# A gate block moved from beside the state output to the start of the glu stage

## The chip, the cores and the metric

The kernel runs on one core of one Trainium2 chip. The metric is device time in microseconds (us) of one launch. The engines are named as the profile names them: PE (TensorE; PEld are its weight loads), ACT (ScalarE), DVE (VectorE), POOL (GpSimd) and SP (SyncE, which here issues nearly all DMAs, in its own order).

## The reference

One inference step of a two-layer hybrid backbone over 128 context and 1024 latent tokens. Cut to what matters here, a layer does this:

```
h = rmsnorm(x, norm_g) * (1 + scale) + shift
a_in, a_gate, f_in, f_gate, q, k, v, c_gate = split(h @ w_in)
ya, finals = s5_mixer(a_in, ...)              # state-space branch, two directions
za = gelu(ya) @ glu_w
ya = za[..., :512] * sigmoid(za[..., 512:])   # the glu stage
yf = fourier_mix(f_in) @ fnet_w
yc = blocked_attention(q, k, v)
branches = stack([ya * silu(a_gate), yf * silu(f_gate), yc * silu(c_gate)])
g = sigmoid(h @ merge_w + merge_b)            # the gates: 3 x 1024 columns
merged = sum(g * einsum(branches, w_branch))
x + gate * (merged @ w_out)
```

The gates `h @ merge_w` need only `h`, so their blocks can be computed at any point of the layer before the branches are merged.

## The kernel before

Activations are kept transposed: 1152 tokens lie along the free dimension in three chunks of 384 (j = 0, 1, 2), channels on the partitions. A dense product is done in blocks of 128 output columns. Each block is a record in a list (weights, right-hand side, evacuation); `dense(n)` takes the next n blocks. Every product is made of three passes with operands split in a high and a low part (`whi`, `wlo` for weights, `hh`, `hl` for h), so four 128-row slices of a weight are 12 matmuls of 384 columns: a **half-chunk**. A gate block (1024 rows) is 6 half-chunks, two for each token chunk; `dense` yields after each. The weights of half a block are one unit: SP loads it into one of four `wst` tiles, ACT makes `whi`, POOL makes `wlo`, and only then is the `wst` tile free for a later load. The products of a chunk gather in one of two PSUM tiles named `pd`; a third chunk can't start before the evacuation of the first.

`drive` interleaves several such generators by weights, `beside(a, b, n)` runs n steps of b after each step of a. Written out so, the work then goes through a scheduler which fixes one order for each engine; the engines run their orders independently and wait on semaphores.

Two neighbouring stages are touched, once in each layer.

**State output** (pool "o"): `ssm_out_gen` goes through eight groups i. For each it makes coefficients on DVE, POOL and ACT (`ss_CA`, `ss_o`, `ss_CK`), a Toeplitz product on PE (`toeplitz`, 16 small matmuls `pt<-ss_CK,ss_B`), evacuates that (`ss_KV` on ACT and DVE), writes it to DRAM (`tpd`), reads it back in another layout (`ss_TT`) and reorders it on ACT (`ss_TP`). One step later `out_gen` uses `ss_TP` as weights: 12 matmuls (`pa` or `pv` from `ssU,ss_TP` and `ss_Hg,ss_CA`), the gelu on ACT (`ss_Y`), and after every second group the DMAs `ydp` and `ydl` that write y to DRAM. Six blocks of gate 0 (`gate_block(0, b, tha)`, evacuated by ACT into a `jo` tile and stored as `tha`) run between these pieces.

**Glu** (pool "u"): `zload_landed` issues 20 DMAs that read y back into twelve `yl` tiles, lets some half-chunks pass, and then makes the high and low copies (`A<-yl` on ACT and on DVE), four of the twelve after each further half-chunk. Beside it runs one block of gate 1 (stored as `thb`). Then come eight glu blocks (`pd<-A,...`, three half-chunks each, alternately evacuated as `th` by ACT and as `jo<-th,pd` by DVE), driven together with `ada_side_gen`, which loads `aw` (512 KB each, three tiles) and accumulates on DVE (`aacc<-aw`, four operations for each load).

Of the kernel before, what the change touches and what calls it, by code (L numbers as in the profile page):

```python
# [89 lines left out]
QT = 20  # L90


def drive(*gens):
    live = [[0.0, g, float(t)] for g, t in gens]
    while live:
        e = min(live, key=lambda x: x[0])
        try:
            e[0] += (next(e[1]) or 1.0) / e[2]
        except StopIteration:
            live.remove(e)  # L100


class Program:
# [1197 lines left out]
    def zload_landed(self, z_d, zf, tag):  # L1301
        ts = []
        for j in range(3):
            for b in range(4):
                t = self.sb(tag, [128, 384], bufs=12, pool=self.gp)
                self.dma_rows(z_d, b, j, t, False)
                ts.append((j, b, t))
        for _ in range(3):
            yield 1
        for i, (j, b, t) in enumerate(ts):  # L1310
            s = slice(384 * j, 384 * j + 384)
            self.act(zf[:, 0, b, s], t)
            self.tt(zf[:, 1, b, s], t, zf[:, 0, b, s].bitcast(F), OP.subtract)
            if i % 4 == 3:
                yield 1
# [40 lines left out]
    def layer(self, l, cs):  # L1356
# [4 lines left out]
        a_d, y_d = ((dt_(n + "p", (512, SP)), dt_(n + "l", (512, SL))) for n in ("ad", "yd"))  # L1361
# [10 lines left out]
        zt = {}  # L1372
# [127 lines left out]
        run = self.run_all  # L1500
# [3 lines left out]
        with self.spool:  # L1504
            with self.epool:
                if l == 0:
                    with self.pool("gp", l, "s"):
                        drive((self.dense(4), 40), (self.ssm_setup_gen(l), 3))
                else:
                    run(self.dense(4))  # L1510
                if l == 0:
                    for k in range(KD):
                        self.dma(self.xT_d[0][128 * k:128 * k + 128, :], self.xT0[:, k])
                with self.pool("gp", l, "m"):
                    drive((self.dense(4), 47), (self.state_gen(l, a_d), 29))
            with self.pool("qp", l):
                with self.pool("gp", l, "q"):
                    self.qkt = self.qkv_tables(l)
                    def qkv():
                        yield from self.qkv_gen(l, qs_d, k_d, v_d, (0,))  # L1520
                        yield from self.qkv_gen(l, qs_d, k_d, v_d, (1,))
                    q = qkv()
                    self.run_some(q, 8)
                    drive((self.scan_gen(l), 103), (self.dense(12), 140))
                    drive((q, 78), (self.dense(2), 21))
                    self.finals(l)
                with self.pool("gp", l, "o"):
                    drive((self.dense(6), 12*6), (self.ssm_out_gen(l, a_d, y_d), 33), (self.qtail_gen(), QT))
        with self.pool("gp", l, "u"):
            zt["y"] = self.sb("A1", [128, 2, 4, NT], R)  # L1530
            run(self.beside(self.zload_landed(y_d, zt["y"], "yl"), self.dense(1), 1))
            drive((self.dense(8), 47), (self.ada_side_gen(l, self.gp, (4, 5)), 6))
        with self.pool("gp", l, "f"):
            self.fnet_tables()
# [81 lines left out]
    def run(self):  # L1616
        self.open_ssm(0)
        cs = self.cs0 = ExitStack()
        self.np_ = cs.enter_context(self.tc.tile_pool(name="np", bufs=1))
        self.xp = cs.enter_context(self.tc.tile_pool(name="xp", bufs=1))  # L1620
        self.prew = []
        self.setup()
        self.xT0 = xT = self.sb("A1", [128, KD, NT])
        ssq = self.ssq = self.sb("ssqt", [128, 2, 9], pool=self.xp)
        self.rb = {}
        self.xr0 = self.sb("xr0", [128, KD, 384], pool=self.xp)
        ada = self.ada_first_gen(0, self.xp, (2, 0, 3, 1))
        xg = self.xg = self.x_gen(xT, ssq)
        next(ada)
        self.run_some(xg, 6)  # L1630
        self.h_tiles((0,))
        self.rb_first(ssq, 0)
        for k in range(KD):
            self.xr_first(xT, k)
        next(ada)
        next(ada)
        for k in range(4):
            self.h_first(xT, 0, k)
        next(ada)
        next(ada)  # L1640
        for k in range(4, 8):
            self.h_first(xT, 0, k)
        self.run_all(ada)
        for l in range(DEPTH):
            with ExitStack() as cs:
                xT, acc = self.layer(l, cs)
                if l + 1 < DEPTH:
                    self.run_all(self.h_gen(l + 1, xT, acc, (2,)))
                else:
                    self.run_all(self.final_gen(xT, acc, (2,)))  # L1650
# [25 lines left out]
```

## Time and profile before

| | |
|---|---|
| median of 3 runs | 2706.3 us (2704.84 to 2707.11) |
| profiled execution, its own time | 2705.34 us |
| span of that execution in the profile | 2703.5 us |
| PE busy | 2598.1 us, 96% of the span |
| DVE, ACT, POOL busy | 1752.9, 1205.0, 666.8 us |
| state output, layer 0 and layer 1 | about 466 to 574 and 1785 to 1896 us |
| glu stage, layer 0 and layer 1 | about 574 to 640 and 1896 to 1962 us |

Every time inside the kernel is counted from the start of the span. Of the 1.84 us between the profiled execution's own time and its span nothing is seen in the trace. The rows of the trace stand in a section of their own below.

### The profile page before, as it was taken

To read this page: it belongs to the slowest core of one execution; us is meant where nothing else is said; L and a number is where in the kernel's file an instruction comes from. 1 tells how busy PE (TensorE), PEld (TensorE's weight loads), DVE (VectorE), ACT (ScalarE), POOL (GpSimd) and SP (SyncE) were. 2 spreads that over 40 slices of the span, in tenths; PEclk is the share of its full clock that TensorE was granted. 3 is DMA by queue.
4 is the path that set the end of the run, shared out by engine and by line. 5 is a ranking of instruction groups with operands and counts; after the bars stand their busy time and mean duration, and the time that the engine had idled before them with its cause. 6 is when DMAs were issued, how large, how long until landed. Compare 5 with 4: busy or idle time off the path is not lost. (4 is left out here: it accounts for less than half of the span.)

```text
span 2703.5 us, 44530 instructions
## 1 busy us (share of the span) xinstructions
PE 2598.1 (96%) x16093; PEld 2496.0 (92%) x16093; DVE 1752.9 (65%) x3837; ACT 1205.0 (45%) x2762; POOL 666.8 (25%) x526
## 2 busy tenths in 40 slices
PE   7999999999999999999999999989999999999998
PEld 4899999899999899999989999979999998999998
DVE  5759964545478889847463798564654787891443
ACT  4562245742355565423345322565223656543244
POOL 2432122312320120222333322232222202101223
PEclk8999999999999999999999999999999999999999
DMA  7633233565443435535542322345646334442234
GB/s 251 199 102 99 86 112 110 168 191 190 157 131 117 141 120 154 186 94 140 170 131 82 116 86 81 119 139 158 209 143 192 104 116 152 146 123 89 89 119 148
DMA packets 463316, 368.95 MB, mean 136 GB/s; under 512 B 72864, under 2 KB 435960, under 8 KB 462712
## 3 DMA queue, kind: packets, MB, share of 16 engines
q1 hardware_dynamic: 461672, 361.78, 43.8%
q0 software_dynamic: 1424, 4.33, 0.5%
q8 instruction: 127, 2.08, 0.3%
q14 instruction: 93, 0.76, 0.1%
HBM read 245.61 MB, written 120.39 MB: 135 GB/s over the span
## 5 line engine op out<-in xcount | busy, mean ns | idle before, releaser
L169 PE MATMUL pd<-hh,whi 128*128 128x384 f32 x2496 | 855.2, 343 | 9.6 <-ACT jo L143 4.9
L169 PE MATMUL pd<-hh,wlo 128*128 128x384 f32 x2496 | 843.6, 338 | 8.3 <-POOL wlo L146 8.1
L169 PE MATMUL pd<-hl,whi 128*128 128x384 f32 x2496 | 840.4, 337 | 1.0 <-DVE hl L150 1.0
L146 POOL TENSOR_TENSOR wlo<-wst,whi 128x512 fp32r<-128x512 f32 x320 | 445.4, 1394 | 1529.9 <-ACT whi L143 1429.7
L169 PEld LDWEIGHTS pd<-hh,whi 128*128 128x128 f32 x2496 | 470.9, 189 | 16.3 <-ACT jo L143 6.5
L169 PEld LDWEIGHTS pd<-hh,wlo 128*128 128x128 f32 x2496 | 470.7, 189 | 14.9 <-POOL wlo L146 13.8
L169 PEld LDWEIGHTS pd<-hl,whi 128*128 128x128 f32 x2496 | 471.2, 189 | 3.8 <-DVE hl L150 2.6
L169 PE MATMUL pd<-A,whi 128*128 128x384 f32 x1728 | 457.1, 341 | 7.0 <-ACT jo L143 6.1
L143 ACT ACTIVATE whi<-wst 128x512 fp32r<-128x512 f32 x320 | 200.6, 630 | 284.7 <-PE pd L169 185.3
L169 PEld LDWEIGHTS pd<-A,whi 128*128 128x128 f32 x1728 | 310.1, 189 | 9.9 <-ACT jo L143 6.7
L169 PE MATMUL pd<-A,wlo 128*128 128x384 f32 x864 | 293.2, 339 | 0.0
L1118 DVE TENSOR_REDUCE at_mx<-pa 128x1 f32<-128x1152 f32 x128 | 173.3, 1354 | 16.0 <-PE pa L169 15.6
L143 ACT ACTIVATE at_PT<-pt 128x384 fp32r<-128x384 f32 (+1 forms) x260 | 114.9, 490 | 143.2 <-PE pt L174 142.8
L169 PE MATMUL pa<-at_K,at_Q 128*128 128x384 f32 x768 | 167.4, 347 | 8.1 <-ACT at_P L143 5.7
L143 ACT ACTIVATE at_P<-pa,at_mx 128x1152 f32<-128x1152 f32 x128 | 158.1, 1235 | 20.5 <-DVE at_mx L1118 19.3
L169 PEld LDWEIGHTS pd<-A,wlo 128*128 128x128 f32 x864 | 162.9, 189 | 0.1
L169 PEld LDWEIGHTS pa<-at_K,at_Q 128*128 128x128 f32 x768 | 128.2, 188 | 28.8 <-ACT at_P L143 25.1
L169 PE MATMUL pt<-qkW,hh 128*128 128x384 f32 x576 | 149.8, 341 | 0.8 <-DVE qk_xn L146 0.8
L169 PE MATMUL pv<-at_PT,at_V 128*128 128x256 f32 x1152 | 148.7, 283 | 0.0
L169 PEld LDWEIGHTS pv<-at_PT,at_V 128*128 128x128 f32 x1152 | 144.7, 191 | 0.8
L143 ACT ACTIVATE jo<-pd 128x384 f32<-128x384 f32 x120 | 58.0, 485 | 189.8 <-PE pd L169 103.2
L146 DVE TENSOR_TENSOR at_PT<-pt,at_PT 128x384 fp32r<-128x384 f32 (+1 forms) x260 | 133.1, 551 | 9.8 <-ACT at_PT L143 9.1
(297 smaller groups left out, 3713.5 us busy)
## 6 DMA issues: line engine op xcount, KB each, us to landing
aw<-in_ada_w_dram SPq DMA_DIRECT2D x48, 512.0 KB, 4.8
wst<-in_merge_w_dram SPq DMA_DIRECT2D x96, 256.0 KB, 3.0
wst<-in_w_in_dram SPq DMA_DIRECT2D x88, 256.0 KB, 3.0
td<-jo SPq DMA_DIRECT2D x96, 192.0 KB, 1.9
jt<-td SPq DMA_DIRECT2D x96, 192.0 KB, 2.6
wst<-in_w_out_dram SPq DMA_DIRECT2D x64, 256.0 KB, 2.9
sgd<-jo SPq DMA_DIRECT2D x72, 192.0 KB, 1.9
jt<-sgd SPq DMA_DIRECT2D x64, 192.0 KB, 3.0
```

The source lines that it names most:

```text
L143: return self.nc.scalar.activation(out, in_, func, **kw)
L146: return (e or self.nc.vector).tensor_tensor(out=out, in0=a, in1=b, op=op)
L169: return self.nc.tensor.matmul(out, w, x, start=first, stop=last, **kw)
L1118: nc.vector.tensor_reduce(out=mx[:, 0:1], in_=src, axis=AX.XY if m3 else AX.X, op=OP.max, negate=True)
```

## The change

In each layer the state output runs beside five blocks in place of six; its weight in `drive` falls from 72 to 60, so a block is worth the same as before. The sixth block (gate 0, b = 7) is taken by the glu stage, which now has two blocks beside the read-back of y; and the copies of y are written two half-chunks further on.

```
@@ -1305,7 +1305,7 @@
                 t = self.sb(tag, [128, 384], bufs=12, pool=self.gp)
                 self.dma_rows(z_d, b, j, t, False)
                 ts.append((j, b, t))
-        for _ in range(3):
+        for _ in range(5):
             yield 1
         for i, (j, b, t) in enumerate(ts):
             s = slice(384 * j, 384 * j + 384)
@@ -1525,10 +1525,10 @@
                     drive((q, 78), (self.dense(2), 21))
                     self.finals(l)
                 with self.pool("gp", l, "o"):
-                    drive((self.dense(6), 12*6), (self.ssm_out_gen(l, a_d, y_d), 33), (self.qtail_gen(), QT))
+                    drive((self.dense(5), 60), (self.ssm_out_gen(l, a_d, y_d), 33), (self.qtail_gen(), QT))
         with self.pool("gp", l, "u"):
             zt["y"] = self.sb("A1", [128, 2, 4, NT], R)
-            run(self.beside(self.zload_landed(y_d, zt["y"], "yl"), self.dense(1), 1))
+            run(self.beside(self.zload_landed(y_d, zt["y"], "yl"), self.dense(2), 1))
             drive((self.dense(8), 47), (self.ada_side_gen(l, self.gp, (4, 5)), 6))
```

No instruction is added or removed. In PE's built order, from one full Toeplitz group (`pt<-ss_CK,ss_B`) to the next there were 48 dense matmuls (four half-chunks) in every period, and 24 before the last nine products of the state output with 72 after them. Now there are 36, 48, 36 and 36 between the groups of steps 4 to 8, 36 between the group of step 8 and the first product of step 9, again 24 before the last nine products, and 144 after them. Both layers have the same order.

On SP, in layer 0, at the write and read-back of the Toeplitz tile of group 6 (`tpd` is its DRAM buffer, `tha` the store of a gate chunk, `wst` a weight unit), there stood before:

```order
L128 DMA tha_374<-jo 128x384
L128 DMA tpd_5352<-ss_KV 1024x1x128
L128 DMA ss_TT<-tpd_5352 128x4x128
L128 DMA tha_374<-jo 128x384
L128 DMA wst<-in_glu_w_dram 128x4x128
```

and now:

```order
L128 DMA tha_374<-jo 128x384
L128 DMA tpd_5352<-ss_KV 1024x1x128
L128 DMA wst<-in_merge_w_dram 128x4x128
L128 DMA ss_TT<-tpd_5352 128x4x128
L128 DMA tha_374<-jo 128x384
L128 DMA wst<-in_glu_w_dram 128x4x128
```

A load of weights now stands between the write and the read-back.

On ACT, in layer 0, where the copies of y begin (the first `jo` is a gate chunk behind the last `ss_Y`; `th` is the first evacuation of the glu), there stood before:

```order
L143 ACTIVATE jo<-pd,hmb_113 128x384
L143 ACTIVATE A_6493<-yl 128x384 x2
L143 ACTIVATE jo<-pd,hmb_113 128x384
L143 ACTIVATE A_6493<-yl 128x384 x2
L143 ACTIVATE whi<-wst 128x512
L143 ACTIVATE A_6493<-yl 128x384 x3
L143 ACTIVATE whi<-wst 128x512
L143 ACTIVATE A_6493<-yl 128x384 x3
L143 ACTIVATE jo<-pd,hmb_113 128x384
L143 ACTIVATE A_6493<-yl 128x384 x2
L143 ACTIVATE th<-pd 128x384 x2
```

and now:

```order
L143 ACTIVATE jo<-pd,hmb_113 128x384
L143 ACTIVATE A_6397<-yl 128x384 x2
L143 ACTIVATE jo<-pd,hmb_113 128x384
L143 ACTIVATE A_6397<-yl 128x384 x2
L143 ACTIVATE whi<-wst 128x512
L143 ACTIVATE A_6397<-yl 128x384 x3
L143 ACTIVATE whi<-wst 128x512
L143 ACTIVATE jo<-pd,hmb_113 128x384
L143 ACTIVATE A_6397<-yl 128x384 x5
L143 ACTIVATE jo<-pd,hmb_113 128x384 x2
L143 ACTIVATE whi<-wst 128x512 x2
L143 ACTIVATE jo<-pd,hmb_113 128x384
```

The third `jo` stands behind seven copies instead of ten, and three more gate chunks follow before the first `th`.

On DVE, in layer 0, behind the low copies of y (`jo<-th,pd` is the first evacuation of the glu that DVE does), there stood before:

```order
L146 TENSOR_TENSOR A_6493<-yl,A_6493 128x384 x12
L371 TENSOR_SCALAR aacc<-aw,silc 128x512 x2
L150 SCALAR_TENSOR_TENSOR aacc<-aw,silc,aacc 128x512 x4
L150 SCALAR_TENSOR_TENSOR jo<-th,pd 128x384
L150 SCALAR_TENSOR_TENSOR aacc<-aw,silc,aacc 128x512
L150 SCALAR_TENSOR_TENSOR jo<-jo,jt 128x384
```

and now:

```order
L146 TENSOR_TENSOR A_6397<-yl,A_6397 128x384 x12
L371 TENSOR_SCALAR aacc<-aw,silc 128x512 x2
L150 SCALAR_TENSOR_TENSOR aacc<-aw,silc,aacc 128x512 x14
L371 TENSOR_SCALAR aacc<-aw,silc 128x512
L377 STREAM_TRANSPOSE aT<-aacc 128x1024
L371 TENSOR_SCALAR aacc<-aw,silc 128x512
L379 TENSOR_REDUCE aR<-aT 128x32
L150 SCALAR_TENSOR_TENSOR aacc<-aw,silc,aacc 128x512 x2
L150 SCALAR_TENSOR_TENSOR jo<-th,pd 128x384
L150 SCALAR_TENSOR_TENSOR aacc<-aw,silc,aacc 128x512
L150 SCALAR_TENSOR_TENSOR jo<-jo,jt 128x384
```

Before the first `jo<-th,pd` there were six operations of the accumulation; now there are 22.

## Rows read from the trace of the kernel before

**Rows 1.** The page's busy time, share of the span and instructions.

```profile
PE 2598.1 (96%) x16093; PEld 2496.0 (92%) x16093; DVE 1752.9 (65%) x3837; ACT 1205.0 (45%) x2762; POOL 666.8 (25%) x526
```

**Rows 2.** PE's waits: start, duration, operation, [idle before, releaser]; layer 0, layer 1.

```profile
590.99 0.61 PE L169 MATMUL pd<-A,whi 128*128 128x384 f32 x2 [2.54 <-ACT jo L143]
604.74 0.62 PE L169 MATMUL pd<-A,whi 128*128 128x384 f32 x2 [0.94 <-DVE jo L150]
...
1825.97 0.52 PE L169 MATMUL pa<-ssU,ss_TP 128*128 128x145 f32 x2 [1.79 <-ACT ss_TP L143]
1887.97 0.52 PE L169 MATMUL pa<-ssU,ss_TP 128*128 128x145 f32 x2 [0.37 <-ACT ss_TP L143]
1913.51 0.88 PE L169 MATMUL pd<-A,whi 128*128 128x384 f32 x2 [3.55 <-ACT jo L143]
```

**Rows 3.** ACT in the glu stage, layer 0, timeline.

```profile
589.42 1.04 ACT L143 ACTIVATE A<-yl 128x384 fp32r<-128x384 f32 x2 [0.99 <-DMA yl<-ydl]
590.37 0.57 ACT L143 ACTIVATE jo<-pd,hmb 128x384 f32<-128x384 f32 x1
```

**Rows 4.** Stretch behind the layer 1 wait: length, busy by engine, PEclk, DMA, GB/s.

```profile
1913.51:1917.26 3.75, 3.75 (x12) 3.75 (x13) 2.62 (x7) 1.15 (x3) 0.00 (x0) 0.54 0.90 301
```

**Rows 5.** PE's timeline, layer 0: two Toeplitz groups, last gate block, first glu matmul.

```profile
529.22 1.02 PE L169 MATMUL pt<-ss_CK,ss_B 128*32 128x240 f32 x16
...
541.70 1.02 PE L169 MATMUL pt<-ss_CK,ss_B 128*32 128x240 f32 x16
...
573.62 0.43 PE L169 MATMUL pd<-hh,whi 128*128 128x384 f32 x1
...
586.20 0.51 PE L169 MATMUL pd<-A,whi 128*128 128x384 f32 x2
```

**Rows 6.** ACT over one period of the state output, layer 0, timeline.

```profile
529.88 0.58 ACT L143 ACTIVATE jo<-pd,hmb 128x384 f32<-128x384 f32 x1
...
530.49 1.06 ACT L143 ACTIVATE ss_CK<-ss_CA 64x448 f32<-64x448 f32 x1
531.44 0.40 ACT L143 ACTIVATE ss_KV<-pt 128x112 f32<-128x112 f32 x2
...
535.33 1.15 ACT L143 ACTIVATE whi<-wst 128x512 fp32r<-128x512 f32 x2
...
541.10 1.12 ACT L143 ACTIVATE ss_TP<-ss_TT 128x512 f32<-128x512 f32 x1 [3.85 <-DMA ss_TT<-tpd]
```

**Rows 7.** SP's issues in the same period.

```profile
532.87 0.53 SPq L128 DMA_DIRECT2D tpd<-ss_KV  x1
537.34 0.38 SPq L128 DMA_DIRECT2D wst<-in_merge_w_dram  x1
537.82 0.46 SPq L128 DMA_DIRECT2D ss_TT<-tpd  x1
```

**Rows 8.** POOL in the same period.

```profile
536.04 2.60 POOL L146 TENSOR_TENSOR wlo<-wst,whi 128x512 fp32r<-128x512 f32 x2 [3.03 <-ACT whi L143]
```

**Rows 9.** DMA issues from 484 to 620 us: count, KB each, median us to landing.

```profile
aw<-in_ada_w_dram SPq DMA_DIRECT2D x8, 512.0 KB, 4.8
tpd<-ss_KV SPq DMA_DIRECT2D x7, 512.0 KB, 4.1
...
ss_TT<-tpd SPq DMA_DIRECT2D x7, 256.0 KB, 3.2
```

**Rows 10.** DVE in the glu stage, layer 0, timeline.

```profile
591.86 0.55 DVE L146 TENSOR_TENSOR A<-yl,A 128x384 fp32r<-128x384 f32 x1
...
597.25 1.41 DVE L150 SCALAR_TENSOR_TENSOR aacc<-aw,silc,aacc 128x512 f32<-128x512 f32 x2 [1.82 <-DMA aw<-in_ada_w_dram]
...
609.45 1.23 DVE L377 STREAM_TRANSPOSE aT<-aacc 128x1024 f32<-128x1024 f32 x1
...
611.32 1.21 DVE L379 TENSOR_REDUCE aR<-aT 128x32 f32<-128x1024 f32 x1
```

**Rows 11.** The `aw` loads from 580 to 620 us: us to landing, least, median and most.

```profile
DMA to landing us min/median/max: 3.7/4.8/5.9
```

More of the change, by code (lines that the diff above doesn't have):

```diff
@@ L1307, in zload_landed @@
                 ts.append((j, b, t))
-        for _ in range(3):
+        for _ in range(5):
             yield 1
@@ L1527, in layer @@
                 with self.pool("gp", l, "o"):
-                    drive((self.dense(6), 12*6), (self.ssm_out_gen(l, a_d, y_d), 33), (self.qtail_gen(), QT))
+                    drive((self.dense(5), 60), (self.ssm_out_gen(l, a_d, y_d), 33), (self.qtail_gen(), QT))
         with self.pool("gp", l, "u"):
             zt["y"] = self.sb("A1", [128, 2, 4, NT], R)
-            run(self.beside(self.zload_landed(y_d, zt["y"], "yl"), self.dense(1), 1))
+            run(self.beside(self.zload_landed(y_d, zt["y"], "yl"), self.dense(2), 1))
             drive((self.dense(8), 47), (self.ada_side_gen(l, self.gp, (4, 5)), 6))
```

## The prediction

> **What bounds the kernel now.** The page's busy times come first: PE is busy for 96% of the span, DVE for 65% [rows 1]. No PE work is added or removed, so the change can move the time only through PE's idle time and its clock. The second view is PE's waits around the two stages [rows 2]. In the glu stage they are 2.54 and 0.94 us in layer 0 and 3.55 us in layer 1. The state output waits for nothing in its steady part in layer 0, and 1.79 and 0.37 us in layer 1. (Both layers also wait once where it begins; the rows used here don't bear on that and I leave it equal.)
>
> The releaser of the two long waits is an evacuation `jo`, and ACT's timeline shows why: that `jo` starts at 590.37, right behind copies of y which had waited for their reads [rows 3]; PE goes on at 590.99. With two `pd` tiles the third chunk can't start before. In layer 1 the granted clock is 0.54 just behind the wait [rows 4], so nearly all of the stretch is at the 1.2 GHz level: 12 matmuls take 3.75 us where 12 should take 2.08, a loss of 1.67 us. Behind the shorter wait of layer 0 there is no such stretch.
>
> **The unit of the sum.** Six half-chunks lie between 573.62 and 586.20 [rows 5]: 2.08 us each, give or take 0.02. One period of the state output is 12.48 us, 529.22 to 541.70 [rows 5]; it holds four half-chunks (8.32) and 4.16 us of its own matmuls.
>
> **Removed: the glu wait.** Call E the end of the state output's last matmul (573.62). Y's low copies end at 591.86 + 0.55 = 592.41 [rows 10], which is E + 18.8. The glu used to begin at E + 12.6; it now begins 12 half-chunks behind E, at E + 25. That leaves 6 us. The new order on ACT must hold too: the third `jo` comes behind seven copies (about E + 14.9) and its tile is wanted at E + 16.7; the fourth comes behind the last copy (E + 18.7) and is wanted at E + 20.8. So this wait goes: -2.54 in layer 0, -3.55 and -1.67 in layer 1. The 0.94 us also goes, being the old order on DVE; what replaces it is counted next.
>
> **Added: DVE's accumulation ahead of the glu.** The built order now puts 22 operations before the first `jo<-th,pd`. The first `aw` loads stand behind three stores of `jo` on SP, the last of which waits for the third `jo`, so they start near E + 16. The median landing of 4.8 us [rows 9, 11] brings the first to E + 21. Each load feeds four operations; two take 1.41 us [rows 10], so 2.8 for four. Four loads end at E + 32.2, if the tiles come free in time (three tiles; the fourth load can start at about E + 23.8, lands at E + 28.6, and is needed at E + 29.4). Then two scalings of some 0.45, the transpose 1.23, the reduction 1.21 [rows 10] and two more accumulations 1.41: E + 37. The evacuation ends at E + 37.5. PE wants that tile at E + 25 plus five half-chunks, E + 35.4. So PE waits 2.1, and with the operations woven between the next evacuations some 0.3 more: 2.4 us in each layer. With the least landing (3.7) it is 1.3, with the most (5.9) 3.5 [rows 11]. Below that stands zero, if the order is no later than the old.
>
> **Moved: six half-chunks out of the state output.** PE's own need from the first product of a step to that of the next falls from 12.48 to 10.4 us where three half-chunks remain (into steps 5, 7 and 8), stays 12.48 into step 6, and is 9.45 into step 9, which has no Toeplitz group. Against it stands the chain that makes `ss_TP`: the evacuation 0.40 and a small DVE operation of about 0.2, `tpd` 4.1 and `ss_TT` 3.2 to landing [rows 9], the reordering 1.1 [rows 6], 9.1 us from `ss_KV` on; and ACT runs other work between one `ss_TP` and the next `ss_KV`. Step by step, from the end of one `ss_TP` to the end of the next, by the built order:
> - Into step 4: about 0.15 over. Into step 5: a weight split and a `jo` first, 1.3, then 9.1 and up to 0.9 behind a store on SP: about 10.85, so 0.45 over.
> - Into step 6: under 10.5 against 12.48, a slack of 2. Into step 7: the DVE operation is queued behind a POOL product that waits for two `wlo` (2.60 for two [rows 8]), 12.3 in all; the slack covers it.
> - Into step 8: a load of weights now stands between `tpd` and `ss_TT` on SP. It waits for `wlo`, which waits for a `whi` behind 6.4 us of ACT work. Before, the same kind of wait is visible: `wlo` starts at 536.04, two take 2.60, and the load goes at 537.34, the read-back only at 537.82, 4.95 us behind its `tpd` [rows 7, 8]. Now: 6.4 + 1.4 + 0.4 for the load + 3.1 + 1.1 = 12.4, against 10.4 and 0.4 of slack left: 1.6 over.
> - Into step 9: `ydp` and `ydl` stand ahead of `tpd`, 9.8 against 9.45: 0.35 over.
>
> Together 2.55 in each layer. In layer 0 nothing stood there, and the split Toeplitz group of step 3 adds some 0.25: +2.8. In layer 1 it takes the place of 1.79 and 0.37, since in step 4 the read-back now stands ahead of the weight load: +0.65 with the 0.25.
>
> Bounds: if the chain fits everywhere, 0 in layer 0 and -2.2 in layer 1. If it stays as long as in this period, 529.22 to 542.22 (541.10 + 1.12) [rows 5, 6], 13.0 us from the start of the Toeplitz group against 11.35 available, the four short steps and the last lose 1.65 four times and 2.6 once: 9.2 in each layer.
>
> The page DMA: Bandwidth & Descriptors of the Trainium skill (Anatomy of one DMA) gives a fitted cost of about 2.0 us plus bytes over 436 GB/s. For 512 KB and 256 KB that is 3.2 and 2.6 us, an estimate by that page; the rows say 4.1 and 3.2 [rows 9]. By the page the steps into 5 and 9 would have no wait and step 8 about 1.1, and the sum would be some 2.6 us lower. The measured landings decide, and the sum goes by them.
>
> **The sum.** Layer 0: -2.54 - 0.94 + 2.4 + 2.8 = +1.7. Layer 1: -3.55 - 1.67 + 2.4 + 0.65 = -2.2. Together -0.5. The profiled execution took 2705.34, of which 2703.5 is the span; the median of the runs is 2706.3, 1.0 above. So the forecast is 2705.8, which I call 2706. What a measurement can tell from no change is 0.2%, 5.4 us.
>
> **Rivals.**
> - *The state output has room and the glu wait is simply gone.* `ss_TP` is in time, as in every steady period of layer 0 now; DVE's early accumulation costs nothing. Then -3.5 and -7.4: -10.9, 2695.5. With half of the DVE wait and 1 us of chain in each layer it is -6.5, 2700. For it: the steady part of layer 0 shows no PE wait at all. Against: in that part ACT itself waits 3.85 us for the read-back [rows 6], and `ss_TP` ends 0.4 us before PE wants it.
> - *The state output's read-back binds in every step (slower).* Place: `tpd`, `ss_TT`, `ss_TP` beside three half-chunks. Price: 9.2 twice, less 2.2, with 0.25 twice for the split group, and -10.9 + 2.2 + 4.8 = -3.9 from the glu: +12.8, 2719. It decides (over +5.4) once the average from Toeplitz group to `ss_TP` is over some 12.3 us, where this period has 13.0. Against: its 13.0 contains 1.4 us of ACT delay and a weight load that three of the five new orders don't have there.
> - *DVE holds the glu longer.* Landings of 5.9 in both layers add 2.2: 2708, still no change.
> - *The wait stays.* If the copies ended later than E + 25, the glu would still wait; they would have to be 6 us later than now, and nothing in the new order delays them.
>
> **How the numbers follow.** The offsetting sum holds 0.53 with 2701 to 2711; roomy state output 0.23 (2694 to 2701); read-back binding 0.24 (2711 to 2720). The range 2698 to 2714 leaves about a tenth on each side. So faster by over 0.2% 0.23, within 0.2% 0.53, slower 0.24.
>
> **What would show it.** Right: no PE wait for `jo` from ACT at the first glu blocks; PE's clock at 1.00 in layer 1 there; a new wait of 1 to 3.5 us for DVE `jo` in the second glu block; waits for `ss_TP` in steps 5, 8 and 9, the longest in step 8, behind an SP load of weights. Wrong: PE waits for `ss_TP` in step 7 or of over 2.5 us; first `aw` landing before E + 19; or a long new wait that sends the clock down again.

## The result and the profile after

The changed kernel takes 2733.6 us (median of 3 runs, 2726.8 to 2736.9) where the kernel before takes 2706.3: a ratio of 1.0096, 95% interval 1.0079 to 1.0114. It is slower, by five times what a measurement can tell, and outside the range of the prediction. The profiled execution is the shortest of the three (2726.8 us, span 2725.1), 21.6 us above the span before.

The page's busy times hardly differ from [rows 1]: PE is 9.2 us busier with the same 16093 instructions.

```profile
PE 2607.3 (96%) x16093; PEld 2505.2 (92%) x16093; DVE 1764.4 (65%) x3837; ACT 1206.2 (44%) x2762; POOL 660.7 (24%) x526
```

So the first question is where PE was idle longer and where it was busy for longer with the same work. Four stretches of each kernel answer it: per layer the state output, from its first Toeplitz product to its last output product, and the glu stage, from the first glu product to the first fnet product (`fn_EO`). The columns are the length, then busy time and count of PE, PEld, DVE, ACT and POOL, the granted clock, DMA share and GB/s. First before, then after; layer 0 state output and glu, layer 1 state output and glu:

```profile
471.28:573.22 101.94, 99.17 (x684) 90.98 (x685) 50.89 (x131) 67.21 (x115) 30.73 (x26) 0.98 0.55 157
586.20:662.01 75.81, 70.40 (x417) 68.46 (x417) 52.99 (x92) 18.69 (x38) 21.30 (x16) 1.00 0.74 238
1790.30:1894.73 104.43, 98.21 (x684) 89.86 (x684) 52.16 (x131) 67.08 (x115) 30.89 (x26) 1.00 0.53 153
1907.71:1984.34 76.63, 71.54 (x417) 70.08 (x417) 53.06 (x93) 19.66 (x40) 21.03 (x16) 0.98 0.74 238
```

```profile
468.65:567.61 98.96, 89.48 (x612) 80.87 (x613) 52.76 (x131) 64.48 (x110) 28.36 (x24) 0.97 0.52 150
593.07:674.32 81.25, 72.61 (x417) 71.43 (x417) 52.15 (x91) 15.77 (x31) 18.15 (x16) 0.94 0.62 196
1800.21:1900.32 100.11, 89.20 (x612) 80.77 (x613) 52.61 (x131) 64.66 (x110) 28.46 (x24) 0.97 0.52 148
1925.78:2008.29 82.51, 73.69 (x417) 72.52 (x417) 52.03 (x91) 15.77 (x31) 16.51 (x16) 0.94 0.60 190
```

The state output has 72 matmuls less, the six half-chunks (12.48 us at the rate of [rows 5]); they come back ahead of the glu, where the gate blocks now take 12.48 us more. With that restored, the stretches have grown by 9.5, 5.4, 8.2 and 5.9 us, 29.0 together. Length less PE's busy time is idle time: it grew by 6.7, 3.2, 4.7 and 3.7 us, 18.4 together. The other 10.6 us (2.8, 2.2, 3.5 and 2.1) are the same matmuls taking longer, and the clock column falls where they do: in these stretches PE is busy at a granted clock of 0.50 to 0.54, its lower level, for 28.0 us, before for 6.9, and half of the difference is 10.6. Of the 7.4 us that keep the span from growing by 29.0, 2.6 lie ahead of the first state output, in code that is the same; the fnet stage gives back 1.3 and 1.5 us, by which PE's next wait, for `fn_EO`, is shorter. The other two runs are 7 and 10 us above the profiled one, so this remainder is no gain of the change.

The waits of PE that are new (they answer to [rows 2]):

```profile
512.90 0.51 PE L169 MATMUL pa<-ssU,ss_TP 128*128 128x145 f32 x2 [3.21 <-ACT ss_TP L143]
549.98 0.52 PE L169 MATMUL pa<-ssU,ss_TP 128*128 128x145 f32 x2 [1.98 <-ACT ss_TP L143]
610.00 1.01 PE L169 MATMUL pd<-A,whi 128*128 128x384 f32 x2 [6.36 <-DVE jo L150]
...
1845.28 0.85 PE L169 MATMUL pa<-ssU,ss_TP 128*128 128x145 f32 x2 [4.37 <-ACT ss_TP L143]
1882.69 0.85 PE L169 MATMUL pa<-ssU,ss_TP 128*128 128x145 f32 x2 [1.98 <-ACT ss_TP L143]
1942.31 1.01 PE L169 MATMUL pd<-A,whi 128*128 128x384 f32 x2 [5.96 <-DVE jo L150]
```

The waits for ACT's `jo` of [rows 2] are gone in both layers, as forecast. In their place stand two waits for `ss_TP` and one of about 6 us for DVE's `jo` per layer. Behind each of them the granted clock falls to its lower level for about 3 to 5 us (the answer to [rows 4]):

```profile
513.90:517.30 3.40, 3.40 (x13) 3.40 (x12) 2.08 (x5) 1.87 (x2) 1.07 (x1) 0.50 0.52 153
551.50:554.80 3.30, 3.30 (x13) 3.30 (x12) 0.23 (x2) 0.38 (x1) 0.00 (x0) 0.50 0.97 275
610.00:612.90 2.90, 2.90 (x9) 2.90 (x10) 2.90 (x6) 0.00 (x0) 0.00 (x0) 0.50 0.66 212
1942.30:1947.50 5.20, 5.19 (x16) 5.20 (x17) 4.89 (x9) 0.63 (x1) 0.51 (x1) 0.50 0.72 223
```

So it does behind the waits for ACT's `jo` at the fnet block that ends the glu stretch (2.28 and 2.85 us, for 3.4 and 3.3 us); before, those waits were 1.93 and 1.54 us and the clock stayed at 1.00.

Why `ss_TP` is late at 512.90, in step 5, stands in the timelines of ACT, DVE and SP. ACT first (against [rows 6]), then DVE:

```profile
500.20 0.42 ACT L143 ACTIVATE ss_KV<-pt 128x112 f32<-128x112 f32 x2
...
511.79 1.06 ACT L143 ACTIVATE ss_TP<-ss_TT 128x512 f32<-128x512 f32 x1 [5.72 <-DMA ss_TT<-tpd]
```

```profile
500.83 1.77 DVE L146 TENSOR_TENSOR ss_CA<-ss_CA,ss_o 128x512 f32<-128x512 f32 x1 [1.18 <-POOL ss_o L146]
502.52 0.22 DVE L150 SCALAR_TENSOR_TENSOR ss_KV<-dmask,ss_D,pt 128x16 f32<-128x16 f32 x1
```

SP, in step 5, then at the write and read-back for step 8, then at the glu stage (against [rows 7]):

```profile
501.89 1.29 SPq L128 DMA_DIRECT2D tha<-jo  x1
503.29 0.52 SPq L128 DMA_DIRECT2D tpd<-ss_KV  x1
...
508.99 0.36 SPq L128 DMA_DIRECT2D ss_TT<-tpd  x1
...
539.96 0.53 SPq L128 DMA_DIRECT2D tpd<-ss_KV  x1
545.14 0.38 SPq L128 DMA_DIRECT2D wst<-in_merge_w_dram  x1
545.63 0.45 SPq L128 DMA_DIRECT2D ss_TT<-tpd  x1
...
584.62 1.09 SPq L128 DMA_DIRECT2D aw<-in_ada_w_dram  x2
```

ACT makes its part of `ss_KV` at 500.2 to 500.6. The small part that DVE makes is done only at 502.74, since the operation ahead of it waited 1.18 us for POOL and then took 1.77. `tpd` goes out 0.55 us after that, behind a store, and its read-back 5.70 us later, when the write has landed. The prediction had 0.2 us for DVE's part and 4.1 for the landing. In layer 1 DVE's part ends 3.4 us behind ACT's, the write goes out 1.6 us later and the read-back 5.44 us behind it.

Step 8 is as predicted: the load of weights between the two goes out only at 545.14, so the read-back follows its write by 5.67 us, though the write had landed after 3.3.

In the glu stage DVE waits for its first `aw`, and then runs 22 operations before the first `jo<-th` (against [rows 10]):

```profile
591.98 1.77 DVE L371 TENSOR_SCALAR aacc<-aw,silc 128x512 f32<-128x512 f32 x2 [4.66 <-DMA aw<-in_ada_w_dram]
593.68 11.44 DVE L150 SCALAR_TENSOR_TENSOR aacc<-aw,silc,aacc 128x512 f32<-128x512 f32 x14
...
609.40 0.54 DVE L150 SCALAR_TENSOR_TENSOR jo<-th,pd 128x384 f32<-128x384 f32 x1
```

The first `aw` is issued at 584.62 and in use 7.4 us later. Of the landing times that the trace has from 570 to 690 us (against [rows 11]) the longest is as long; it belongs to the load issued at 588.41.

```profile
DMA to landing us min/median/max: 3.6/3.9/7.4
```

### The profile page after: what moved, and what is told of

It reads as the page before. It is cut to its first block, busy times and chain, and to the rows that moved or that the text cites. A ratio compares the mean times of both kernels' runs of the same rounds, so it can differ in the third digit from the quotient of the medians.

```text
span 2725.1 us, 44524 instructions
## 1 busy us (share of the span) xinstructions
PE 2607.3 (96%) x16093; PEld 2505.2 (92%) x16093; DVE 1764.4 (65%) x3837; ACT 1206.2 (44%) x2762; POOL 660.7 (24%) x526
## 5 line engine op out<-in xcount | busy, mean ns | idle before, releaser
L169 PE MATMUL pd<-hh,whi 128*128 128x384 f32 x2496 | 857.3, 344 | 11.2 <-ACT jo L143 6.5
L146 POOL TENSOR_TENSOR wlo<-wst,whi 128x512 fp32r<-128x512 f32 x320 | 438.7, 1372 | 1545.6 <-ACT whi L143 1444.7
L169 PE MATMUL pd<-A,whi 128*128 128x384 f32 x1728 | 458.4, 342 | 12.3 <-DVE jo L150 12.3
```

The lines of the kernel that those rows point to most:

```text
L146: return (e or self.nc.vector).tensor_tensor(out=out, in0=a, in1=b, op=op)
L169: return self.nc.tensor.matmul(out, w, x, start=first, stop=last, **kw)
```

## Experiments

The theory after the result, called M below, is that of separate costs: the state output lacks half-chunks to cover its read-back, DVE's sums stand ahead of the glu's first evacuation, and each long wait brings half-rate matmuls. Ratios are to the kernel before, run on the same chip, with 95% intervals. "State" and "glu" are the lengths of the stretches above, layer 0 and layer 1.

```text
run                  ratio  [95% interval]    state          glu
before                                        101.9 104.4    75.8 76.6
changed              1.0096 [1.0079, 1.0114]   99.0 100.1    81.3 82.5
e1_copies_early      1.0081 [1.0068, 1.0094]   98.1  99.9    75.8 76.0
e2_glu_alone         1.0042 [1.0029, 1.0055]  101.8 103.2    (block gone from fnet)
e3_output_alone      1.0039 [1.0027, 1.0051]  (begins otherwise)  74.7 77.4
e4_sums_later        1.0040 [1.0026, 1.0055]   98.2 102.0    73.9 74.1
e5_block_from_attn   1.0106 [1.0088, 1.0123]  101.8 102.4    74.5 73.9
e6_no_round_trip     1.0027 [1.0017, 1.0037]   91.6  93.7    79.8 78.8
e7_half_step         1.0128 [1.0107, 1.0149]  100.2 101.6    78.9 78.3
e8_aw_first          1.0051 [1.0036, 1.0065]   99.9  99.4    73.8 75.3
e9_no_u_loads        1.0050 [1.0037, 1.0063]   95.5  98.5    78.3 80.8
e10_late_copies      0.9998 [0.9990, 1.0007]  101.7 104.6    75.6 76.8
e11_before_tuned     1.0013 [1.0004, 1.0022]  101.7 103.7    77.8 77.7
e12_block_from_scan  1.0053 [1.0039, 1.0068]  101.7 101.8    75.3 76.2
e13_late_copies_sums 1.0008 [0.9998, 1.0017]  102.0 103.9    78.7 78.3
e14_all_taken_out    0.9994 [0.9984, 1.0004]   91.5  92.7    76.6 76.5
```

### One side alone

**e2.** The state output keeps six blocks; the glu's second block comes from the fnet stage.

```diff
+  dense_add([gate_block(1, b, thb) for b in range(2)])   # before the glu blocks
-  run(beside(zload_landed(y_d, zt["y"], "yl"), dense(1), 1))
+  run(beside(zload_landed(y_d, zt["y"], "yl"), dense(2), 1))   # and range(5) in zload_landed
   # fnet stage
-  run(self.dense(1))
```

> State output with six blocks as before the change; the glu stage begins with two gate blocks and y's copies are traced after five half-chunks as in the changed kernel; the second block is taken from the beginning of the fnet stage, where one was run by itself. Theory M: the state output costs what it did before, the glu stage (first glu product to first fnet product) loses a block of 12.5 us and keeps the wait of about 6 us for DVE's jo with half-rate matmuls behind it, 5.4 to 5.9 us per layer over the kernel before: 2716 us, up to 2724 if the fnet stage then waits for what its block covered. Rival A (nearly all of the slowdown is made on the glu side): 2725 to 2737. Rival B (all of it is made in the state output, the glu wait is a mere substitute for the old one): 2702 to 2708.

Measured 2717.1 us, as M has it. The state output has none of the new waits for `ss_TP`; DVE's wait is there, and a new one where the fnet stage gave up its block (the profile names no releaser for it):

```profile
611.96 1.01 PE L169 MATMUL pd<-A,whi 128*128 128x384 f32 x2 [5.50 <-DVE jo L150]
...
670.14 0.56 PE L169 MATMUL pv<-fn_EO,dftc 128*128 128x2 f32 x2 [5.99 <-issue]
```

**e3.** The state output alone with five blocks, the sixth ahead of it.

```diff
-  drive((self.dense(6), 12*6), (self.ssm_out_gen(l, a_d, y_d), 33), ...)
+  run(self.dense(1))
+  drive((self.dense(5), 60), (self.ssm_out_gen(l, a_d, y_d), 33), ...)
```

> Only the state output changed: five gate blocks beside it, the sixth run by itself just ahead of it, the glu stage as before the change. Theory M: the state output loses 9.5 us in layer 0 and 8.2 us in layer 1 to waits for ss_TP (steps 5 and 8 the longest) and to half-rate matmuls behind them, the glu stage has its old waits of 2.5 and 3.6 us: 2720 to 2726 us. Rival A (glu side): 2704 to 2710. Rival B (state output alone): 2726 to 2736.

Measured 2716.3 us, under M's 2720 but far from A and B. Its waits for `ss_TP` are 5.1 us at the first output products, where the block ahead also changed the order, then 2.5 and 2.2 us in layer 0. The two halves together (12.7 and 11.8 us above before) are about the whole (22.7 in e1, 27.3 in the changed kernel), but partly by luck: in e2 PE's waits in the fnet stage are some 3 us longer than before in each layer, and e3's first wait belongs to its own order. What they show is that neither side makes the slowdown alone.

**e1.** The block moved, y's copies left where they were: `range(3)` in place of `range(5)`.

> The changed kernel with y's copies traced after three half-chunks again, so that only the block is moved. Theory M (two costs, of the moved block alone: too few half-chunks between the Toeplitz products and the output products of the state output, and the DVE sums in front of the glu stage's first evacuation): no difference to the changed kernel, 2726 to 2737 us, waits of 3 to 4.4 us for ss_TP in step 5 and of about 6 us for DVE's jo. Rival C (the copies' place itself costs something, because ACT or SP reach the loads of the glu weights and the aw tiles later): the DVE wait shrinks by the 2 to 3 us by which the first aw landed later than I had reckoned, in both layers, and the time falls by 4 to 7 us.

Measured 2727.2 us; its interval overlaps the changed kernel's. The trace decides more than the total does: DVE's wait did shrink, and another came back.

```profile
587.39 0.44 PE L169 MATMUL pd<-hh,whi 128*128 128x384 f32 x1 [1.76 <-ACT jo L143]
609.38 0.61 PE L169 MATMUL pd<-A,whi 128*128 128x384 f32 x2 [1.39 <-DVE jo L150]
```

The gate blocks, now behind ACT's copies again, take 3.6 and 3.9 us longer (29.1 and 29.3 us in place of 25.5), so PE reaches the glu later and waits less there. Counted from the end of the last output product (E, 567.61 + 0.40 in the changed kernel, 568.32 + 0.40 here), PE goes on at E + 40.7 where the changed kernel does at E + 42.0. DVE's sums end at nearly the same place whatever PE does ahead of them. Theory C's shrinking wait was seen, but not for its reason: SP issues the first `aw` later, not earlier (E + 19.0, in the changed kernel E + 16.6), and DVE uses it at E + 23.5 where the changed kernel has E + 24.0.

### The glu side: sums, and the load they wait for

**e4.** The sums depend on a copy of `silc` written after the third evacuation.

```diff
+  if (b, j) == (0, 2):                       # in the glu evacuation
+      self.silc2 = self.sb("silc2", [128, KD, 2], pool=self.gp)
+      self.stt(silc2, o[:, :2 * KD], 0.0, silc, OP.mult, OP.add)
-  w = self.silc[:, 2 * k + h, c:c + 1]
+  w = (self.silc if silc is None else silc)[:, 2 * k + h, c:c + 1]   # silc=self.silc2
```

> The changed kernel, with the DVE sums (aacc from aw) made to depend on the third evacuation of the first glu pair by a copy of silc that is written there (one small DVE instruction more per layer), so that no sum can stand ahead of the first evacuations. Theory M: the 6 us waits for DVE's jo go, with the half-rate stretch behind them, and no other wait takes their place; the stage from the first glu product to the first fnet product falls from 81 to 72 or 73 us in each layer, the total by 14 to 18 us, to 2710 to 2720. Rival A': something else is late at the same place (y's last copies, jt, th), the wait changes its name and the time falls by under 5 us, to 2722 to 2734.

Measured 2715.7 us, as M has it: the glu stage falls to 73.9 and 74.1 us (M: 72 or 73), PE's waits for DVE there are 1.04 us at most, the clock 1.00.

```profile
592.96:666.89 73.93, 70.74 (x418) 68.49 (x418) 49.84 (x85) 15.76 (x31) 21.26 (x16) 1.00 0.65 207
1927.30:2001.44 74.14, 70.63 (x418) 68.49 (x418) 49.70 (x85) 15.76 (x31) 20.60 (x16) 1.00 0.65 209
```

**e8.** The sums stay where they are; only the first two loads of `aw` go out earlier.

```diff
+  aw = {u: self.ada_load(l, self.gp, 3, 4, u) for u in range(2)}
   run(self.beside(self.zload_landed(y_d, zt["y"], "yl"), self.dense(2), 1))
-  drive((self.dense(8), 47), (self.ada_side_gen(l, self.gp, (4, 5)), 6))
+  drive((self.dense(8), 47), (self.ada_side_gen(l, self.gp, (4, 5), ld=aw), 6))
```

> The changed kernel, with the first two loads of aw issued ahead of the reads of y in place of behind the first glu weights. Theory M (of the wait of 6.4 us for DVE's jo, 4.7 us are the late landing of the first aw, the rest the sums themselves): DVE starts the sums right behind its last copy of y, the wait falls to 1.5 to 2 us in both layers and the half-rate stretch behind it goes: 6 to 7 us per layer, 12 in all, ratio to before 1.004 to 1.006. Rival G (the loads delay y): y lands 2 to 5 us later, the wait moves to the first glu products or to ACT's jo in the gate blocks, and under 5 us in all are won.

Measured 2717.9 us, ratio 1.0051, as M has it. The wait falls to 1.66 us in both layers, and 4.7 us of 6.4 were the load:

```profile
607.21 0.62 PE L169 MATMUL pd<-A,whi 128*128 128x384 f32 x2 [1.66 <-DVE jo L150]
...
1935.21 0.61 PE L169 MATMUL pd<-A,whi 128*128 128x384 f32 x2 [1.66 <-DVE jo L150]
```

607.21 is E + 37.6 here. The prediction had this evacuation end at E + 37.5 with the loads behind three stores; it comes true only with the loads in front.

### The state output: the round trip

**e6.** The read of a step's tile is taken from the tile of the step before, so that the chain to `ss_TP` has a step more.

```diff
-  self.dma(Tt, tp_d[i].rearrange(...))
+  self.dma(Tt, tp_d[max(i - 1, 0)].rearrange(...))
```

> The changed kernel, with ss_TT read from the tile that was written to tpd one step earlier (for the first step, its own), so that the read does not wait for this step's write to land; the numbers of the state output are then wrong, the amount of work is the same. Theory M (the chain Toeplitz product, ss_KV, write, landing, read, landing, ss_TP of some 15 us is longer than a step with three half-chunks): the waits for ss_TP of 3.2 and 2.0 us in layer 0 and 4.4 and 2.0 us in layer 1 go, with the half-rate matmuls behind them; from first Toeplitz to last output product 90 us in place of 98 to 100; the total falls by 14 to 18 us against the changed kernel, to a ratio to before of 1.002 to 1.004. Rival E (ss_TP is late because ACT gets to it late, not because of the transfers): the waits stay above 1.5 us each and the total falls by under 6 us.

Measured 2711.4 us, ratio 1.0027: all later waits for `ss_TP` are gone, only those of 1.0 and 2.2 us at the first output products and one for `ss_Y` (1.46 and 0.70 us) are left. The state output takes 91.6 and 93.7 us; six blocks less one would be 89.5 and 92.0. So most of that side's cost is that the chain from the Toeplitz product to `ss_TP` has one step and not two. Which link of it is late e6 can't tell: from the fourth group on the reads go out 3.4 to 5.6 us behind the write of the tile before and 5 to 9 us ahead of their own step's write, so that DVE's late part of `ss_KV` no longer counts either. ACT's late turn (rival E) is out already by the changed kernel's own trace, where ACT waits 5.72 and 3.81 us for the read-backs of steps 5 and 8.

**e9.** Two of four loads of `ssU` left out.

```diff
-  U[x // 2] = self.u_load(a_d, x // 2)
+  U[x // 2] = self.u_load(a_d, x // 2) if x < 4 else U[x // 2 - 2]
```

> The changed kernel, with the third and fourth loads of ssU left out (adp and adl are not read again, the tiles of the first two are used in their place), so that the state output's second half is wrong and its transfers are fewer. Theory M1 (the long wait for ss_TP in step 5 comes from the transfers that stand in front of tpd's write on SP and run beside it: the write issued 2.4 us after its data were ready and took 5.7 us): the wait falls from 3.2 and 4.4 us to under 1.5 us in both layers, those of step 8, at 2.0 us, stay; 3 to 5 us per layer with the half-rate matmuls, ratio to before 1.006 to 1.008. Rival M2 (the chain is as long without them, since y's writes, tha's and the weight loads stay in the bunch): the wait stays above 2.5 us, ratio 1.008 to 1.010.

Measured ratio 1.0050, more gain than either forecast. PE's waits in layer 0, and SP's issues:

```profile
512.00 0.51 PE L169 MATMUL pa<-ssU,ss_TP 128*128 128x145 f32 x2 [1.09 <-ACT ss_TP L143]
547.54 0.52 PE L169 MATMUL pa<-ssU,ss_TP 128*128 128x145 f32 x2 [1.98 <-ACT ss_TP L143]
```

```profile
503.66 0.52 SPq L128 DMA_DIRECT2D tpd<-ss_KV  x1
...
508.09 0.36 SPq L128 DMA_DIRECT2D ss_TT<-tpd  x1
```

Step 5's wait falls from 3.21 to 1.09 us in layer 0 and from 4.37 to 2.28 in layer 1 (M1 had under 1.5 in both), step 8's stays at 1.98. The 2.1 us of layer 0 are three parts: DVE's part of `ss_KV` is 0.3 us less late, the write goes out at once in place of 0.55 us later, and the read-back follows it by 4.43 us in place of 5.70. In layer 1 the parts are 0.1, 1.0 and 1.0. What is left of the wait has DVE's part still 1.8 and 3.3 us behind ACT's; no run takes that away. Of the whole gain, 3.0 and 1.7 us lie in the glu stretches, which the edit leaves alone.

How far one trace can be trusted here, e1, e4 and e8 tell, whose state output has the changed kernel's order on every engine: step 5 waits 1.90, 1.95 and 3.60 us in layer 0 and 3.9 to 4.0 in layer 1, step 8 always 1.9 to 2.0. Step 7 waits 1.7 to 1.8 us in layer 0 in all three, where the changed kernel's trace has no wait.

**e7.** Coefficients in the first half of a step, its Toeplitz products at the middle.

```diff
-  if 1 <= x < 9: toeplitz(x - 1)             # at a step's beginning
+  if q == 2 and x < 8: toeplitz(x)           # at its third quarter
-  next(cg, None)
+  if q < 2: next(cg, None); next(cg, None)
```

> The changed kernel, with the coefficients of a step made in its first half and its Toeplitz products put at the middle of the step in place of the next step's beginning, half a step (some 5 us) ahead of where they were against the output products that read them. Theory M: the round trip gets 5 us more, the 2 to 4.4 us waits for ss_TP shrink below 1 us; the total falls by 10 to 16 us against the changed kernel, ratio to before 1.003 to 1.005. Rival F (the coefficients or their engines then come last): waits for ss_CK ahead of the Toeplitz products take their place and the total falls by under 5 us, ratio 1.007 to 1.010.

Rival F in kind, though the time is above its range and no gain is left. The late waits for `ss_TP` go, and waits for `ss_CK` of 2.1 to 2.9 us, three per layer, take their place (one of them below); ratio 1.0128. The chain ahead of the Toeplitz products has no more room than the one behind them.

```profile
535.33 0.61 PE L169 MATMUL pt<-ss_CK,ss_B 128*32 128x240 f32 x8 [2.87 <-ACT ss_CK L143]
```

### Can another stage spare the block?

**e5** and **e12** give the glu its second block and held sums, leave the state output its six, and take the block elsewhere.

```diff
-  yield from self.dense(5)      # e5, attention stage (the fnet blocks one further on)
+  yield from self.dense(4)
-  drive((self.scan_gen(l), 103), (self.dense(12), 140))   # e12, scan stage
+  drive((self.scan_gen(l), 103), (self.dense(11), 128))
```

> State output with six blocks as before; glu stage with two blocks at its beginning, y's copies after five half-chunks, and the DVE sums held back until after the third evacuation; the second block is taken from the attention stage, the fnet stage keeps its one. Theory M (each stage pays for its own cover): the state output as before, no wait for ACT's jo and none of 6 us for DVE's jo in the glu stage, so 74 us from the first glu to the first fnet product where the kernel before has 75.8 and 76.6: 4 to 5 us faster than before, ratio 0.998, if the attention stage can spare the block. Rival D (a block is cover wherever it stands): the attention stage loses some of the 12.5 us that the block ran for, and the kernel is slower than before, up to a ratio of 1.008.

> State output with six blocks as before; glu stage with two blocks, y's copies after five half-chunks and the DVE sums held back; each layer's second block is in effect taken from the scan stage, which runs eleven blocks in place of twelve. From the kernel that took it from the attention stage, the two layers' stretches from the state output to the fnet stage are worth 1.5 and 4.8 us. Theory M (what a block is worth depends on the stage that gives it up): if the scan stage has work of its own for PE all along, ratio 0.997 to 0.998. Rival D (every stage needs its blocks): the scan stage waits for DVE or ACT by 5 to 12 us per layer, ratio 1.002 to 1.007.

Rival D both times. State output and glu are as good as forecast, 74 to 76 us in the glu, but the stage that gave the block does not get shorter by its 12.5 us, since it now waits: attention for `at_P`, by up to 3.8 us in each layer, the scan for `qk_xn` by over 9. From the last fnet product to the next state output, or to the end, e5 takes 0.5 and 7.9 us longer than before, and its ratio is above D's range; from the start, or the last fnet product, to the state output e12 takes 3.9 and 1.7 us less. First e5, then e12:

```profile
1116.00 1.51 PE L174 MATMUL pt<-ident,at_P 128*128 128x128 f32 x6 [3.81 <-DVE at_P L1122]
```

```profile
348.84 1.01 PE L169 MATMUL pt<-qkW,hh 128*128 128x384 f32 x2 [9.69 <-DVE qk_xn L146]
...
1678.28 1.01 PE L169 MATMUL pt<-qkW,hh 128*128 128x384 f32 x2 [9.44 <-DVE qk_xn L146]
```

### Was the old wait worth what it lasted?

**e10** and **e11** leave the blocks as before and trace y's last four copies behind the gate block; e11 also issues `aw` first, by the lines of e8.

```diff
+  if i == 8:
+      self.last = lambda: [cp(*x) for x in ts[8:]]
+      return
   # glu stage, behind the gate block
+  self.last()
   drive((self.dense(8), 47), (self.ada_side_gen(l, self.gp, (4, 5)), 6))
```

> The kernel before, its blocks where they were; only the last four of the twelve copies of y are traced behind the gate block in place of within it, so that ACT's jo for that block stands ahead of them. Theory M (the wait for ACT's jo at the glu stage's beginning, 2.5 and 3.6 us with half rate behind the second, is ACT's order of work and needs no further block): the wait shrinks to under 1 us in both layers, 4 to 6 us in all, ratio to before 0.998. Rival H (the third chunk of the first glu block then waits for its copies): the wait changes its name to A, under 2 us in all, ratio 0.9995 to 1.0005.

> The kernel before with the late copies and with the first two loads of aw issued ahead of the reads of y. Theory M: as the late copies alone, and DVE's wait of 0.9 us at the second glu block goes as well: ratio to before 0.997 to 0.998. Rival G (the loads of aw push y's reads back, which here have only one block beside them): y's copies come 2 to 3 us later and PE waits for A or for jo at the first glu products, ratio 0.999 to 1.001.

In e10 the waits for ACT's `jo` fall to 0.88 us in both layers, and the time doesn't (ratio 0.9998): there are two waits for DVE's `jo` of 0.94 us per layer (before, one in layer 0), and in layer 1 one for ACT's `th` of 0.70. The ratio is rival H's, though the new waits are not for y's copies. In e11 (1.0013, a little above G's range) PE waits for y's low copies instead, rival G:

```profile
587.19 0.62 PE L169 MATMUL pd<-A,whi 128*128 128x384 f32 x2 [0.88 <-ACT jo L143]
...
602.80 0.61 PE L169 MATMUL pd<-A,whi 128*128 128x384 f32 x2 [0.94 <-DVE jo L150]
```

```profile
588.32 0.44 PE L169 MATMUL pd<-A,whi 128*128 128x384 f32 x1 [2.45 <-DVE A L146]
```

**e13** is e10 with e4's held sums; **e14** is the changed kernel with e4's held sums and e6's read, so that its two costs are out.

> The kernel before with y's last four copies behind the gate block and with the DVE sums held back until after the third evacuation of the first glu pair, the blocks where they were. Theory M (the waits at the glu stage's beginning are worth what they last: 2.5 and 0.9 us in layer 0, 3.6 us and 1.7 us of half rate in layer 1; in the kernel with late copies alone DVE's two waits of 0.9 us per layer gave them back): both kinds go, and the stage from the first glu to the first fnet product falls from 75.8 and 76.6 to 73.5 or 74 us; 4 to 5 us in all, ratio to before 0.998 to 0.9985. Rival I (PE's waits there are filled by what follows, so that taking them away wins nothing): 75 us or more in each layer, ratio 0.9995 to 1.0005.

> The changed kernel with the DVE sums held back and with the read of tpd one step behind its write, so that both costs of the change are out and only its gain is left (the state output's numbers are wrong for the second). Theory M (the costs add, and the gain booked for the removed wait is real): the state output 2 us per layer over what it was before less one block, as without the round trip alone, the glu stage at 74 us, 1.9 and 2.5 us under before; in all about even, ratio to before 0.9990 to 1.0005. Rival J (the costs overlap: half of what one takes away the other brings back): ratio 1.002 to 1.004.

e13 falls to rival I: ratio 1.0008, the glu stage longer (78.7 and 78.3 us). The copies that no longer stand ahead of `jo` stand ahead of `th`:

```profile
586.50 0.62 PE L169 MATMUL pd<-A,whi 128*128 128x384 f32 x2 [0.68 <-ACT jo L143]
590.11 0.62 PE L169 MATMUL pd<-A,whi 128*128 128x384 f32 x2 [1.25 <-ACT th L143]
```

e14 comes out even, 0.9994, as M has it: 1.9 us under before (interval 4.3 under to 1.1 over). So the two costs together are the whole slowdown. How much of the gain is left, the traces don't settle. The glu stage, forecast at 74 us, takes 76.6 and 76.5 in e14, 0.6 us more than before in the two layers together; with the same glu stage e4, e5 and e12 are 4.4, 4.1 and 0.9 us under before. The mean of the four is 2.2 us where the prediction booked 8.7. Part of the spread is the wait at the fnet block, 1.2 and 1.5 us in e4, 2.4 and 2.3 with half-rate matmuls behind it in e14. No version tried beats the kernel before beyond its interval.

## Why the prediction was wrong

- **The glu wait goes: right.** The glu begins at E + 25, and no wait for ACT's `jo` is left at its first blocks. Its worth was put too high: -8.7 us booked, 2.2 found on average where the new costs of the glu stage are out (e4, e5, e12, e14), and nothing in e10 and e13, where other waits came in its place.
- **DVE's accumulation ahead of the glu: right in kind, wrong in size.** The step that failed is "the median landing of 4.8 us brings the first to E + 21". The first `aw` was in use at E + 24.0 (7.4 us), and sixteen operations took 13.1 us where 11.2 had been reckoned. The wait was 6.36 and 5.96 us where 2.4 was forecast: 7.5 us of the error. e8 and e4 take it away, by the load and by the order of the sums. The bound of 5.9 us was the most seen around that stage in one trace; after the change a landing took 7.6 us in layer 1.
- **The state output: two steps bind, one of them for more than its price.** Into step 8 the prediction had 1.6 over, behind the load of weights; it measured 1.98 in both layers, for that reason. Into step 5 it had 0.45 over, and 3.21 and 4.37 were measured. Two terms of that step failed: DVE's part of `ss_KV`, "a small DVE operation of about 0.2", ended 2.1 and 3.4 us behind ACT's, and the landing of `tpd`, 4.1 us taken, was 5.7 and 5.4. A late DVE operation behind POOL was in the prediction, but for step 7. Step 6 had slack; step 7 waited in e1, e4 and e8, and step 9 in e8 (0.67). Idle time grew by 11.4 us where 3.45 was forecast. e6 shows that the chain to `ss_TP` binds, e9 that part of step 5's wait, 2.1 us in its trace, comes with the loads of `ssU`. The rival of a binding read-back had the right size for the wrong reason: its 9.2 us per layer, spread over five steps, against 9.5 and 8.2 measured, of which 6.7 and 4.7 are idle time, most of it in two steps, and the rest clock.
- **The clock: no term.** I booked the removed half-rate stretch (-1.67 us) and none for the new waits, though a long new wait that sends the clock down stood in the list of what would make the forecast wrong. It is the largest part of the error: 10.6 us more of PE's busy time, so 12.3 us off.
- **The sum.** -0.5 forecast, +29.0 measured in the stretches. The difference is 7.5 for DVE, 8.0 for the idle time of the state output, 12.3 for the clock and 1.7 for the longer waits at the fnet block.

The prediction weighed a fitted cost of the Trainium skill's page DMA: Bandwidth & Descriptors (Anatomy of one DMA), 3.2 us for 512 KB, an estimate by it. The Trainium skill's page states that fit for transfers issued from GpSimd, and `tpd` goes out on SP. The estimate is farther from the 5.70 us of step 5 with the `ssU` loads, and from the 4.43 without, than the row of before.

What stays open: why the first `aw` took 7.4 us (it follows twenty reads of y, three stores and a weight load; issued 2.4 us later in e1 it came at nearly the same moment, and e8 moved it, but no run took its neighbours away); how much of step 5's wait DVE's late part alone makes; and why the clock fell behind some waits and not behind others.

## What to carry to other kernels

A block of matmuls that waits for nothing is the cover of whatever chain runs beside it: price its removal by the chain it uncovers (every engine that makes the tile, write, landing, read, landing, copy), step by step, and look for the step where one of these engines is late or other transfers land in company. Here every stage asked to give one up paid in waits of its own: state output, attention and scan for most of the block, fnet for some 3 us per layer. Take a transfer's time from the moment it will run in, not from its median; and give every new wait of 2 us or more a term for the half-rate matmuls that may follow.

## What was not expected of the hardware

- After PE waits of 2.0 to 6.4 us the matmuls ran at the 1.2 GHz level for about 3 to 5 us, not always from the restart: behind 512.90 the granted clock is 1.00 until 513.9 and 0.50 from there to 517.3, behind 549.98 it is 0.50 from 551.5 on. In the kernel before, 2.54 us of waiting in layer 0 [rows 2] had no such stretch, and waits of 1.30 and 0.70 us at its first Toeplitz products had one (0.50 from 473.3 to 476.6).
- DVE's sums took 0.82 us each in a row of fourteen (11.44 us), where two took 1.41 in [rows 10]. Twelve of the fourteen took 0.74 us and two 1.78; these two, at 594.34 and 600.68, are the only ones that begin while POOL makes a `wlo`. In the whole trace seven of the 29 sums beside a POOL operation took over 1 us, and none of the other 83. The late `ss_CA` of step 5 (1.77 us, 0.69 where POOL is idle) begins beside a `wlo` too, at 500.83. No run tests the cause. First the sums from 570 to 690 us (duration in ns, least, median and most), then POOL:

```profile
L150 DVE SCALAR_TENSOR_TENSOR aacc<-aw,silc,aacc x28: 736/740/1781, 593.7 to 620.5; 128x512 f32<-128x512 f32 x28
```

```profile
593.87 1.70 POOL L146 TENSOR_TENSOR wlo<-wst,whi 128x512 fp32r<-128x512 f32 x1 [0.79 <-ACT whi L143]
600.09 1.82 POOL L146 TENSOR_TENSOR wlo<-wst,whi 128x512 fp32r<-128x512 f32 x1 [4.53 <-ACT whi L143]
```

- Runs of one kernel spread over 10 us and more (e4: 2707.9 to 2722.8). The length of a stretch with the same order varies less, but not by nothing: the state output in layer 0 takes 98.1, 98.2, 99.0 and 99.9 us in e1, e4, the changed kernel and e8, the glu stage with held sums 73.9 to 76.6 us in e4, e5, e12 and e14. A difference of 2 or 3 us between two single traces shows nothing by itself.
